# Product keys folded into the query's weights ahead of time, beside the token mixers

## Chip, core and metric

One core of a Trainium2 chip runs the kernel. The metric is the device time of one execution in microseconds (us), the median over several runs. PE is TensorE (PEld its weight loads), DVE VectorE, ACT ScalarE, POOL GpSimd, SP SyncE. SP, ACT and POOL issue DMAs, each from a queue of its own that works in program order; 16 DMA engines move the bytes.

## What is computed

One trunk layer on 1024 tokens of 1024 channels, float32. Two causal mixers (an RG-LRU and an S5) read one projection of the normalized input, their joint output is projected and added to the residual, and a product-key expert layer (PEER) follows:

```python
def block(xb):                                   # 128 tokens of the normalized h
    q = (xb @ wq).reshape(TOK_BLOCK, 8, 256)     # 8 heads, two halves of 128
    s1 = einsum('thd,kd->thk', q[..., :128], k1) # 128 keys each
    s2 = einsum('thd,kd->thk', q[..., 128:], k2)
    v1, i1 = top_k(s1, 16)
    v2, i2 = top_k(s2, 16)
    sc, cidx = top_k(all pairs v1 + v2, 16)
    e = expert numbers of the 16 pairs; g = softmax(sc)
    act = gelu(einsum('thkd,td->thk', u_tab[e], xb))
    return einsum('thk,thkd->td', g * act, v_tab[e])
```

For one half, `s = (xb @ wq_n) @ k.T`, which is also `xb @ (wq_n @ k.T)`: the product of the weights with the keys does not depend on the tokens.

## The kernel before

Products that need float32 accuracy are made of three matmuls in a faster type: a tile x is split into a high part (a rounded copy, made by ACT) and a low part (x less the high part, made by DVE), and low x high, high x low and high x high are summed in PSUM.

The program has four stages. **Mixers** (`front`, to about 250 us): input projection (`usp`, `pj`), S5 by quarters (`quarter`), the LRU heads (`lru`), then the GLU. Weights of the projection come in through SP's queue, nine pairs of parts ahead (`WBUFS`); two tiles `T0` hold the S5 kernel matrices; POOL clears them once at the start and does nothing until it loads the residual `h` for the output projection (L841). **Output projection** (`w_out`, `wop`), which also normalizes `h` for the expert layer (`Norm2`). **Query** (`query`, L1016): the tokens are 3 gathered blocks (TG = 384 tokens) and 5 dense blocks (TD = 640). For each of 16 column tiles of wq, first for the gathered blocks and then again for the dense ones, a 512 KB tile `wqr` is loaded by SP and split into `wqh` and `wql`; 24 matmuls (`qp`) of 384 columns, or 48 of 320, give the query in channel-by-token form, ACT copies it (`qt`), and for each block and half a float32 matmul with the keys `kT` gives the scores (`sp`). The first tile is made earlier, in `query0` (L880). Scores of the gathered blocks stay on chip (`sc`), those of the dense blocks go to DRAM (`S_d`) and are loaded back as `s` by `topk`. DVE's `top16` (MAX, MAX_INDEX, MATCH_REPLACE) finds 16 of 128 (`vg`, `ixg` for gathered blocks; `v`, `ix` for dense ones), then 16 pairs (`cd`, `scv`, `ci`).
**Experts**: for the gathered blocks, POOL fetches 128 rows of u and 128 of v for each block by indirect DMA (`row`), and DVE multiplies them with the tokens; the rows needed are spread over the rest of the program. For the dense blocks, all 128 x 128 experts are computed: tiles of u are loaded and split (`ur`, `uh`, `ul`), `ap` is the first matmul, `gp` builds the weights from one-hot products, `vp` is the second matmul.

The order of the work is decided when the program is built. Each strand (`proj`, `quarter`, `lru`, `query`, ...) is a generator that yields between pieces, and `Merge` (`mg`) runs the one whose modelled time plus a bias is least; `mg.at(t)` sets a strand's earliest time, `mg.dma(kb)` models a load, `mg.flag` and a yielded name let one strand wait for another. Each engine then carries out its instructions in the order that results, and an instruction whose operand isn't there holds up all that stand behind it on its engine. `fps` is the PSUM pool of `front`: 4 banks `pt`, 2 `pj`, 2 `pu`.

Of the kernel before, what the change touches and what calls it, by code (L numbers as in the profile page):

```python
# [149 lines left out]
def front(tc, a, cst, nd, mg):  # L150
# [28 lines left out]

    pvt = pools.open("fvt")  # L180
# [41 lines left out]
    pw = pools.open("fw", "right", bufs=9)  # L222
# [8 lines left out]
    WBUFS = 9  # L231
# [257 lines left out]
    def quarter(q):  # L489
# [42 lines left out]
        T0 = T0s[q % 2]  # L532
# [99 lines left out]
    mg.run([(0.5, proj_first())], until="us0")  # L632
# [26 lines left out]
    def lru(m):  # L659
# [18 lines left out]
        tau = pl.tile([P, T], F32, name="tau", tag="tau")  # L678
# [23 lines left out]
        V.tensor_tensor(tau, tau, i_, ALU.mult)  # L702
        yield
        V.tensor_tensor_scan(x, r_, tau, 0.0, ALU.mult, ALU.add)
# [93 lines left out]
    def wo_half(half):  # L798

        for n in range(2):  # L800
            for k in range(4):
                if half:
                    yield "half0" if (n, k) >= (1, 2) else "cols0"
                r = po.tile([P, 512], F32, name="wor", tag="wor", bufs=2)
                nc.sync.dma_start(r, a["w_out"][(4 * half + k) * P:(4 * half + k + 1) * P, 512 * n:512 * n + 512])
                wh = po.tile([P, 512], F32R, name="woh", tag="woh", bufs=10)
                wl = po.tile([P, 512], F32R, name="wol", tag="wol", bufs=10)
# [70 lines left out]
    nx = Norm2(tc, a, cst, pools, h, ss, mg)  # L878

    def query0():  # L880

        hi, lo = [], []
        for i in range(2):
            r = po.tile([P, 512], F32, name="wor", tag="wor", bufs=2)
            nc.sync.dma_start(r.rearrange("p (k n) -> p k n", n=P), a["wq"][0][:, 4 * i:4 * i + 4])
            yield "half0"
            wh = po.tile([P, 512], F32R, name="woh", tag="woh", bufs=10)
            wl = po.tile([P, 512], F32R, name="wol", tag="wol", bufs=10)
            S.activation(wh, r, AF.Copy)
            V.tensor_tensor(wl, r, wh.bitcast(F32), ALU.subtract)  # L890
            hi += [wh[:, k * P:(k + 1) * P] for k in range(4)]
            lo += [wl[:, k * P:(k + 1) * P] for k in range(4)]
            yield
        yield "xg"
        yield "half1"
        p_ = pt("qp")[:, :TG]
        for k in range(8):
            PE.matmul(p_, hi[k], nx.xGl[:, k], start=(k == 0), stop=False)
            PE.matmul(p_, lo[k], nx.xGh[:, k], start=False, stop=False)
            PE.matmul(p_, hi[k], nx.xGh[:, k], start=False, stop=(k == 7))  # L900
        yield
        S.activation(nx.q0, p_, AF.Copy)
        mg.flag("query0")
# [958 lines left out]
```

## Time and profile before

| | us |
|---|---|
| median of 3 runs (2582.36 to 2586.19) | 2584.22 |
| the profiled execution | 2589.38 |
| its span, first to last instruction | 2587.6 |

The profile is of one execution. Busy times are of matmuls in a pipeline whose ends are modelled, so a busy PE isn't PE at its peak: two matmuls overlap, and the step from one to the next is shorter than the duration listed. A group's row reads: line, engine, operation, out<-in, shapes, count, busy us, mean ns of one, idle time of the engine just before them and what ended most of it. L146 is the helper that records all compute instructions, so groups are told apart by their tiles. In the chain, each row is a start, a length and what ran, followed back from the last instruction. DMA share is the mean busy share of the 16 engines. The mean granted clock of PE over the span was 0.991.

### The profile page before, as it was taken

How to read it: one execution, taken by the hardware profiler on the slowest of the kernel's cores; microseconds unless marked ns; L12 is line 12 of the kernel's file. 1: busy time of each engine (PE TensorE's matmuls, PEld its weight loads, DVE VectorE, ACT ScalarE, POOL GpSimd, SP SyncE). 2: the span in 40 equal slices, each digit the busy share in tenths (PEclk: the TensorE clock that was granted, in tenths of full speed). 3: DMA queues.
4: the chain of work that ended last, by engine and by line, in shares of the span. 5: the costliest groups of instructions: out<-in, count | busy, mean ns of one | idle time of the engine just before them, and what ended most of it. 6: DMA issues, size and time to landing. Idle time of an engine off the chain costs nothing.

```text
span 2587.6 us, 40757 instructions
## 1 busy us (share of the span) xinstructions
PE 2493.5 (96%) x14623; PEld 2255.7 (87%) x14623; DVE 2364.6 (91%) x4556; ACT 1331.8 (51%) x2402; POOL 1149.4 (44%) x785
## 2 busy tenths in 40 slices
PE   7998999998999999999999999999999999999997
PEld 6776778998999999999999988888888888888886
DVE  7899559997999999999977599999999999999998
ACT  5566434332467777777877444334443443334442
POOL 0000000243466465574655365555556566555551
PEclk9999999998999999999999999999999999999999
DMA  5113223586799999998999999999999999999994
GB/s 180 35 42 100 72 92 123 178 289 234 275 364 347 345 337 361 348 327 310 355 380 345 343 382 359 355 359 351 350 350 373 349 357 355 355 353 351 348 355 152
DMA packets 303354, 752.78 MB, mean 291 GB/s; under 512 B 29872, under 2 KB 128368, under 8 KB 298416
## 3 DMA queue, kind: packets, MB, share of 16 engines
q0 software_dynamic: 111744, 406.90, 43.1%
q1 hardware_dynamic: 186576, 336.28, 36.4%
q10 hardware_dynamic: 4832, 7.00, 0.8%
q8 instruction: 115, 1.88, 0.3%
q14 instruction: 87, 0.71, 0.1%
HBM read 662.92 MB, written 85.98 MB: 289 GB/s over the span
## 4 chain that ended last, share of the span: by engine, by line
PE 60%; DVE 20%; issue 3%; DMA 2%; ACT 1%; POOL 1%; another core or an unknown queue 0%; DVEq 0%; SPq 0%; ACTq 0%; POOLq 0%
PE vp L146 26%; PE ap L146 19%; PE total L146 6%; PE qp L146 4%; DVE row L146 3%; PE gp L146 3%; DVE hb L146 3%; DVE ul L146 2%; DVE oh L146 2%; DVE ix L146 1%; DVE ohA L146 1%; DVE v L146 1%; PE wop L146 1%; DVE s L146 1%; DVE ci L146 1%
## 5 line engine op out<-in xcount | busy, mean ns | idle before, releaser
L1290 POOL DMA_INDIRECT row<-in_peer_u_dram,idx x384 | 579.1, 1508 | 691.8 <-DVE scv L146 268.7
L1290 POOL DMA_INDIRECT row<-in_peer_v_dram,idx x384 | 563.1, 1466 | 452.8 <-DVE hb L146 278.7
L146 PE MATMUL ap<-xDl,uh 128*128 128x320 f32 x2048 | 647.8, 316 | 5.0 <-ACT aa L146 5.0
L146 PE MATMUL ap<-xDh,ul 128*128 128x320 f32 x2048 | 639.6, 312 | 8.8 <-DVE ul L146 8.6
L146 PE MATMUL ap<-xDh,uh 128*128 128x320 f32 x2048 | 636.9, 311 | 0.0
L146 DVE SCALAR_TENSOR_TENSOR hb<-row,act,hb 128x1024 f32<-128x1024 f32 x384 | 494.9, 1289 | 4.9
L146 DVE CUSTOM_DVE_ANT_0 row<-row,xg 128x1024 f32<-128x1024 f32 x384 | 459.0, 1222 | 4.3 <-DMA row<-in_peer_u_dram,idx 4.3
L146 PEld LDWEIGHTS ap<-xDh,ul 128*128 128x128 f32 x2048 | 388.7, 190 | 11.9 <-DVE ul L146 10.8
L146 PE MATMUL vp<-vl,hh 128*128 128x512 f32 x1024 | 398.7, 389 | 0.0
L146 PE MATMUL vp<-vh,hl 128*128 128x512 f32 x1024 | 398.5, 389 | 0.0
L146 PE MATMUL vp<-vh,hh 128*128 128x512 f32 x1024 | 398.5, 389 | 0.0
L146 PEld LDWEIGHTS ap<-xDl,uh 128*128 128x128 f32 x2048 | 388.5, 190 | 7.8 <-ACT aa L146 6.6
L146 PEld LDWEIGHTS ap<-xDh,uh 128*128 128x128 f32 x2048 | 388.2, 190 | 0.0
L146 ACT ACTIVATE gq<-gt 128x640 f32<-128x640 f32 x128 | 174.7, 1365 | 319.1 <-DVE hr L146 253.7
L146 PEld LDWEIGHTS vp<-vh,hh 128*128 128x128 f32 x1024 | 192.2, 188 | 40.2
L146 PEld LDWEIGHTS vp<-vl,hh 128*128 128x128 f32 x1024 | 192.2, 188 | 39.4 <-issue 0.4
L146 PEld LDWEIGHTS vp<-vh,hl 128*128 128x128 f32 x1024 | 192.2, 188 | 38.8
L146 ACT ACTIVATE ohB<-ohB,kt 128x128 f32<-128x128 f32 x480 | 202.1, 485 | 0.0
L146 ACT ACTIVATE aa<-ap 128x320 f32<-128x320 f32 x194 | 84.4, 435 | 207.9 <-PE ap L146 198.7
L146 PE MATMUL gp<-ohB,ohA 128*128 128x128 f32 x1280 | 173.1, 278 | 15.7 <-DVE ohB L146 13.8
L146 PEld LDWEIGHTS gp<-ohB,ohA 128*128 128x128 f32 x1280 | 159.2, 192 | 25.4 <-issue 13.1
L146 DVE TENSOR_TENSOR ul<-ur,uh 128x1024 fp32r<-128x1024 f32 x128 | 156.6, 1224 | 21.2 <-ACT uh L146 21.2
(445 smaller groups left out, 4500.2 us busy)
## 6 DMA issues: line engine op xcount, KB each, us to landing
ur<-in_uT_dram SPq DMA_DIRECT2D x128, 512.0 KB
vr<-in_peer_v_dram SPq DMA_DIRECT2D x128, 512.0 KB
gt<-G_d SPq DMA_DIRECT2D x32, 1280.0 KB
G_d<-gs SPq DMA_DIRECT2D x79, 512.0 KB
A_d<-aa SPq DMA_DIRECT2D x96, 320.0 KB
hr<-A_d SPq DMA_DIRECT2D x96, 320.0 KB
wqr<-in_wq_dram SPq DMA_DIRECT2D x31, 512.0 KB
row<-in_peer_u_dram,idx POOLq DMA_INDIRECT x384
```

The costliest lines, as they stand in the source:

```text
L146: return fn(*args, **kw)
L1290: G.indirect_dma_start(out=r, out_offset=None, in_=a["peer_v" if at >= P else "peer_u"], in_offset=bass.IndirectOffsetOnAxis(ap=idx[n][:, ...
```

## The change

The keys are multiplied into the query's weights once, by a new strand `fold` that runs beside the mixers. It takes the transposed weights in 32 units of 256 KB (128 query channels by 512 input channels). For each unit a tile `wqr` (two buffers) is loaded through POOL's queue, four float32 matmuls with `kT` give `fo` (512 columns), ACT copies the high part into `wqh` (one buffer), DVE writes the low part over `wqr`, and POOL's queue stores both into `W_d` in DRAM. `BEAT` is the distance of two units in the builder's time.

```diff
+    def fold():
+        kT = pfo.tile([P, 2, P], F32, name="kT")
+        nc.gpsimd.dma_start(kT, a["kT"])
+        units = [(n, i) for n in range(16) for i in range(2)]
+        ready = []
+        def load():
+            n, i = units[len(ready)]
+            r = pfo.tile([P, 512], F32, name="wqr", tag="wqr", bufs=2)
+            nc.gpsimd.dma_start(r, a["wqT"][n][:, 512 * i:512 * i + 512])
+            ready.append((r, mg.dma(256)))
+        load()
+        for at, (n, i) in enumerate(units):
+            if at + 1 < len(units):
+                load()
+            r, t = ready[at]
+            mg.at(t + 1.0)
+            yield
+            t = mg.cur["t"]
+            p_ = pu("fo")
+            for j in range(4):
+                PE.matmul(p_[:, j * P:(j + 1) * P], r[:, j * P:(j + 1) * P], kT[:, n % 2], start=True, stop=True)
+            yield
+            hi = pfo.tile([P, 512], F32R, name="wqh", tag="wqh")
+            lo = r.bitcast(F32R)
+            S.activation(hi, p_, AF.Copy)
+            V.tensor_tensor(lo, p_, hi.bitcast(F32), ALU.subtract)
+            yield
+            for m, x in enumerate((hi, r)):
+                nc.gpsimd.dma_start(nx.W_d[m, n // 4, :, n % 4, 4 * i:4 * i + 4].bitcast(F32),
+                                    x.bitcast(F32).rearrange("p (k n) -> p k n", n=P))
+            mg.at(t + BEAT)
+            yield
+        mg.flag("fold")
-    mg.run([(0.5, proj_first())], until="us0")
+    mg.run([(0.5, proj_first()), (FOLD, fold())], until="us0")
```

The query then gives scores at once: tokens are the stationary side, and a quad of four column tiles (two heads, 512 scores) the moving one, so each of 768 matmuls has 512 columns; `sp`, `qt` and the split leave the stage. Its weights come from `W_d` by SP, a high and a low tile of 1 MB for half of the input channels of a quad, one step ahead; `query_head` does the first half quad on tiles loaded during the output projection. Scores of a block leave as 512 columns (`S_d`, 256 KB).

```diff
-                        for k in range(8):
-                            PE.matmul(p_, wh[:, k], dl[:, k, sl], start=(k == 0), stop=False)
-                            PE.matmul(p_, wl[:, k], dh[:, k, sl], start=False, stop=False)
-                            PE.matmul(p_, wh[:, k], dh[:, k, sl], start=False, stop=(k == 7))
-                        if i == 0 and at < 31:
-                            nxt = weights(at + 1)
...
-                    for f in range(2):
-                        PE.matmul(p_[:, f * P:(f + 1) * P], qs[f][:, n * P:(n + 1) * P], kT[:, f], start=True, stop=True)
...
+            for c in range(4):
+                held = nx.held if part + c == 0 else [nx.bank() for _ in blocks]
+                for j in range(1 if part + c == 0 else 0, 2):
+                    load()
+                    wh, wl = ready.pop(0)
+                    for n, b in enumerate(blocks):
+                        for k in range(4):
+                            nx.term(held[n], dh, dl, n, 4 * j + k, wh[:, :, k], wl[:, :, k])
                         yield
...
+                        if j:
+                            sc = pq.tile([P, 512], F32, tag="sc", name="sc", bufs=3)
+                            S.activation(sc, held[n], AF.Copy)
+                            if part:
+                                nc.sync.dma_start(S_d[b, :, 2 * c:2 * c + 2], sc.rearrange("p (h k) -> p h k", h=2))
```

To make room, the mixers keep one `T0` instead of two, eight weight pairs ahead instead of nine, eight `woh`/`wol` buffers instead of ten, and `lru` uses the tiles of `x` and `xc` for `tau` and `x`. PSUM pool `fps` stays open until the query is done.

```diff
-    WBUFS = 9
+    WBUFS = 8
-    T0s = [p5.tile([P, 8, P], F32, name=f"T0{i}") for i in range(2)]
-    for x in T0s:
-        G.memset(x, 0.0)
+    T0 = p5.tile([P, 8, P], F32, name="T0")
+    G.memset(T0, 0.0)
-        tau = pl.tile([P, T], F32, name="tau", tag="tau")
+        tau, x = x, xc
```

How it stands on the engines. POOL's queue during the mixers, before (`T0` are the cleared tiles, `h` the residual's blocks):

```order
L146 MEMSET T00_538 128x1024
L146 MEMSET T01_539 128x1024
L841 DMA h7_2457<-in_x_dram 128x1024
L841 DMA h6_2456<-in_x_dram 128x1024
L841 DMA h5_2455<-in_x_dram 128x1024
```

and now, the first units of the fold (`wqr_550`, `_625` and `_552`, `_682` are the same two buffers in turn):

```order
L635 DMA kT_548<-in_kT_dram 128x256
L642 DMA wqr_550<-in_wqT_dram 128x512
L642 DMA wqr_552<-in_wqT_dram 128x512
L146 MEMSET T0_546 128x1024
L662 DMA W_d_97<-wqh_570 128x512
L662 DMA W_d_97<-wqr_550 128x512
L642 DMA wqr_625<-in_wqT_dram 128x512
L662 DMA W_d_97<-wqh_632 128x512
L662 DMA W_d_97<-wqr_552 128x512
L642 DMA wqr_682<-in_wqT_dram 128x512
```

The load of a third unit now stands between the stores of the first and those of the second, and it can't start before the store of the first unit's `wqr` has left; the eight loads of `h` stand behind the last store.

DVE in the first half of the query stage, before, where the low parts of the weights stand between the searches of the gathered blocks:

```order
L146 MAX vg_3360<-sc 128x8 x2
L146 MAX_INDEX ixg_3361<-vg_3360,sc 128x8 x2
L146 TENSOR_TENSOR wql<-wqr,wqh 128x1024
L146 MAX vg_3362<-sc 128x8 x2
L146 MAX_INDEX ixg_3363<-vg_3362,sc 128x8 x2
L146 MATCH_REPLACE sc<-vg_3362,sc 128x128 x2
L146 MAX vg_3362<-sc 128x8 x2
L146 MAX_INDEX ixg_3363<-vg_3362,sc 128x8 x2
L146 TENSOR_TENSOR wql<-wqr,wqh 128x1024
```

and DVE now in the mixers, where the fold's low part has come between the S5 and LRU instructions:

```order
L146 TENSOR_TENSOR wqr<-fo,wqh 128x512
L146 SCALAR_TENSOR_TENSOR xa_74<-r__1143,i__1144 128x1024
L146 SCALAR_TENSOR_TENSOR xc<-xa_75,cols,xc 128x1024
L146 TENSOR_TENSOR wqr<-fo,wqh 128x512
L146 SCALAR_TENSOR_TENSOR xc<-xa_75,cols,xc 128x1024 x2
L146 TENSOR_TENSOR Wr<-inr,Ec 128x4x127
L146 TENSOR_TENSOR xt<-ini,Es 128x4x127
```

The 31 full-width `wql` have left the query stage, and 32 half-width `wqr` stand among the mixers.

SP's queue at the end of the query stage, before:

```order
L1023 DMA wqr<-in_wq_dram 128x1024 x2
L1067 DMA S_d<-sc 128x256 x5
L1023 DMA wqr<-in_wq_dram 128x1024
L1067 DMA S_d<-sc 128x256 x10
L1115 DMA s<-S_d 128x2048
```

and now:

```order
L1068 DMA wq_5199<-W_d 128x4x512
L1090 DMA S_d<-sc 128x512
L1068 DMA wq_5197<-W_d 128x4x512
L1090 DMA S_d<-sc 128x512
L1140 DMA s<-S_d 128x2048
L1090 DMA S_d<-sc 128x512 x4
```

The first dense block's scores `s` are now read back ahead of the stores of the other four blocks.

More of the change, by code (lines that the diff above doesn't have):

```diff
@@ L178, in front @@
     S.dma_start(cols, a["cols"])
+    nx = Norm2(tc, pools)
+    pfo = pools.open("ffold")
     pvt = pools.open("fvt")
@@ L701, in lru @@
         yield
-        V.tensor_tensor(tau, tau, i_, ALU.mult)
+        V.tensor_tensor(i_, tau, i_, ALU.mult)
         yield
-        V.tensor_tensor_scan(x, r_, tau, 0.0, ALU.mult, ALU.add)
+        V.tensor_tensor_scan(tau, r_, i_, 0.0, ALU.mult, ALU.add)
         yield
@@ L877, in front, with bank, query_head @@
     pools.close("fa")
[L878 to L893, printed above, removed]
+    nx.open(a, cst, pools, h, ss, mg)
+    used = [0]
+    def bank():
+        used[0] += 1
+        return (pt if used[0] % 6 < 4 else pj)("qp")
+    nx.bank = bank
+    def query_head():
+        yield "fold"
+        w = []
+        for m in range(2):
+            x = pvt.tile([P, 4, 4, P], F32R, name="wq0", tag="Vt", bufs=2)
+            nc.sync.dma_start(x.bitcast(F32), nx.W_d[m, 0, :, :, 0:4].bitcast(F32))
+            w.append(x)
         yield "xg"
         yield "half1"
-        p_ = pt("qp")[:, :TG]
-        for k in range(8):
[L898 to L903, printed above, removed]
+        nx.held = [bank() for _ in range(NG)]
+        for n, p_ in enumerate(nx.held):
+            for k in range(4):
+                nx.term(p_, nx.xGh, nx.xGl, n, k, w[0][:, :, k], w[1][:, :, k])
+            yield
+        mg.flag("head")
     def norm2_g():
@@ L1012, in norm2_d, with load @@
     def norm2_d():
-        yield from nx.run(dblocks, xDh, xDl, pt)
+        yield from nx.run(dblocks, xDh, xDl, nx.pu)
         mg.flag("xd")
     def query():
-        kT = pq.tile([P, 2, P], F32, name="kT", bufs=1)
-        S.dma_start(kT, a["kT"])
-        def weights(n):
-            wr = pq.tile([P, 8, P], F32, tag="wr", name="wqr")
-            nc.sync.dma_start(wr, a["wq"][n % 16])
-            wh = pq.tile([P, 8, P], F32R, tag="wh", name="wqh")
-            wl = pq.tile([P, 8, P], F32R, tag="wl", name="wql")
-            split_to(wh, wl, wr)
-            return wh, wl
-        nxt = weights(1)
+        quads = [(part, c, j) for part in range(2) for c in range(4) for j in range(2)][1:]
+        ready = []
+        def load():
+            if quads:
+                _, c, j = quads.pop(0)
+                w = []
+                for m, tag in enumerate(("wh", "wl")):
+                    x = pq.tile([P, 4, 4, P], F32R, name="wq2", tag=tag)
+                    nc.sync.dma_start(x.bitcast(F32), nx.W_d[m, c, :, :, 4 * j:4 * j + 4].bitcast(F32))
+                    w.append(x)
+                ready.append(w)
+        load()
         yield
         for part, (blocks, dh, dl) in enumerate(((gblocks, nx.xGh, nx.xGl), (dblocks, xDh, xDl))):
-            nt = len(blocks) * P
-            nsp = -(-nt // 512)
-            w = nt // nsp
             if part:
@@ L1491, in peer @@
     mg.run([(1.0, topks()), gr], until="q")
+    pools.close("fps")
+    ppa = pools.open("ppa", bufs=2, space=PSUM)
+    ppt = pools.open("ppt", bufs=2, space=PSUM)
     mg.run([], until="chosen")
```

83 lines of the change are left out of this document (34 added, 49 removed).

## The prediction

> **What bounds the kernel now.** First the page's busy times, then the busy time of each engine by stage (stretch in us, its length, then PE, PEld, DVE, ACT, POOL busy, granted clock, DMA share, GB/s), since one share over the whole span mixes stages.
>
> ```profile
> PE 2493.5 (96%) x14623; PEld 2255.7 (87%) x14623; DVE 2364.6 (91%) x4556; ACT 1331.8 (51%) x2402; POOL 1149.4 (44%) x785
> ...
> 50.00:228.00 178.00, 163.78 (x1073) 127.60 (x1071) 166.79 (x290) 107.62 (x164) 0.00 (x0) 0.98 0.15 38
> 250.00:371.00 121.00, 113.37 (x505) 91.51 (x504) 65.54 (x98) 43.69 (x64) 2.52 (x5) 0.97 0.24 88
> 371.00:611.00 240.00, 228.67 (x1498) 220.84 (x1497) 212.93 (x800) 85.00 (x164) 61.97 (x44) 0.99 0.61 207
> 605.00:1050.00 445.00, 425.98 (x2941) 416.95 (x2940) 437.54 (x1250) 288.32 (x680) 236.06 (x152) 0.98 0.90 321
> 1050.00:1440.00 390.00, 383.24 (x2753) 379.23 (x2752) 350.50 (x746) 303.75 (x736) 229.65 (x140) 1.00 0.97 347
> 1440.00:2588.00 1148.00, 1130.05 (x5583) 977.71 (x5582) 1076.62 (x1230) 459.60 (x516) 614.57 (x433) 0.99 0.93 344
> ```
>
> The mixers (50 to 228) keep PE busy for 163.8 of 178 us and DVE for 166.8: both are nearly full, POOL does nothing, and DMA moves 38 GB/s. The output projection (250 to 371) is PE's. The query stage (371 to 611) is shared by PE and DVE; DVE has 27 us free in it. From 605 to 1050 DVE is full (437.5 of 445), and from there to the end PE is. The order in which DVE stands is the same in both kernels from the 25th expert tile on, so a shift that DVE has when it reaches that stage goes through to the end. The question is therefore how much later the mixers end and how much shorter the query stage becomes. The chain of work that ended last shows where the query stage goes (start us, us, what):
>
> ```profile
> 352.03 19.07 PE wop L146 x84
> 371.11 3.92 DMA wqr<-in_wq_dram
> ...
> 454.12 7.30 PE qp L146 x42
> ...
> 493.29 1.14 DVE wql L146
> ...
> 499.43 4.45 DMA row<-in_peer_u_dram,idx
> ...
> 554.61 13.06 PE qp L146 x89
> 567.66 0.89 PE sp L146 x8
> ...
> 602.33 3.46 DMA S_d<-sc
> 605.86 5.13 DMA s<-S_d
> ```
>
> The stage begins with a wait for the first weights (371.11), which could only be loaded when the projection had left its buffers. In its first half the low parts of the weights (wql) stand among the top-16 searches on DVE; in the second PE runs alone, and at its end DVE waits 8.6 us until the scores have gone to DRAM and come back.
>
> **The query stage: what goes.** Matmul steps come from that chain: 512 columns 19.07/84 = 0.227 us, 384 columns 7.30/42 = 0.174, 320 columns 13.06/89 = 0.147, and a record of a score matmul 0.89/8 = 0.111. Before: 384 x 0.174 + 768 x 0.147 = 179.7 us of projection. After: 768 x 0.227 = 174.3. So the projection stays, and the 128 score matmuls (two records each) leave:
>
> ```profile
> L146 PE MATMUL sp<-kT,qt 128*128 128x128 f32 x250 | 38.6, 284 | 3.1 <-ACT qt L146 2.1 <-ACT sc L146 1.0
> ...
> L146 DVE CUSTOM_DVE_ANT_0 row<-row,xg 128x1024 f32<-128x1024 f32 x36 | 43.4, 1225 | 2.8 <-DMA row<-in_peer_u_dram,idx 2.8
> L146 DVE TENSOR_TENSOR wql<-wqr,wqh 128x1024 fp32r<-128x1024 f32 x31 | 37.7, 1217 | 4.6 <-ACT wqh L146 4.5
> ```
>
> With the 6 of the first tile these are 256 records x 0.111 = 28.4 us of PE. DVE loses 31 wql at a step of 1.14 = 35 us, and 7 of the 36 gathered rows move behind the stage (29 stand ahead of the first dense search in the new order), 7 x 1.22 = 8.5 us that are paid back in the DVE-bound stage. What is left: PE 174.3 + 40 transposes x 0.11 = 179 us, DVE 213 - 35 - 8.5 = 169 us.
>
> New here are the loads. A step takes two tiles of 1 MB (2.1 MB together), twice the bytes of before. For the gathered blocks a step lasts 36 x 0.227 = 8.2 us, and 2.1 MB at 347 GB/s (stretch 1050:1440) take 6.0, with some 3 until they land (the 4.45 of a gathered row of 512 KB less 1.5 for its bytes): about 1 us is missing at each of 7 steps, so PE ends at 179 + 8 = 187 us after 371. For the dense blocks (480 matmuls, 109 us) the DMA engines must move 16.8 MB of weights, 5.2 MB of scores and 29 to 36 rows of 0.52 MB: 37 to 41 MB, 107 to 118 us at 347 GB/s. I take it that the rows, not the weights, are late, and that DVE comes to the first dense search 10 us after PE's end, at 197. The wait for S_d nearly goes: block 0's scores are stored and read back while PE still works on four blocks. Before, that search began at 611, 240 us in: **-43 us**, and +8.5 for the rows. Bounds: -53 (DVE there when PE ends) to -32 (41 MB at the 321 GB/s of 605:1050, 128 us after the first 80).
>
> **The mixers: what comes.** 32 units: 4 matmuls (8 records x 0.111 = 0.89 us), one high part on ACT, one low part on DVE, three DMAs on POOL's queue. The nearest rows for the two parts read PSUM in the same form, 128x512:
>
> ```profile
> L146 DVE TENSOR_TENSOR xDl<-x2t,xDh 128x512 fp32r<-128x512 f32 x10 | 6.8, 676 | 0.0
> L146 ACT ACTIVATE xDh<-x2t 128x512 fp32r<-128x512 f32 x10 | 5.9, 596 | 4.4 <-PE x2t L146 4.3
> ```
>
> PE gets 32 x 0.89 = 28.5 us, DVE 32 x 0.6 to 0.68 = 19 to 22, ACT 19 (it has 70 free). PE had 14 us free from 50 to 228, DVE 11. So the least is 28.5 - 14 = +14 us on PE (DVE: 19 - 11 = +8), the work being pushed into every gap.
>
> On top comes the round of a buffer. A unit's low part is written over its raw tile, so the tile is free for the load two units on only when the store of the low part has left, and POOL's queue holds that load with the next unit's stores behind it. A round is a load (4.45 us for 512 KB from the chain, 3.7 less the time of half its bytes), 0.89 + 0.60 + 0.68, and a store (3.46 in the chain): 9.3 to 10.1 us; I take 10. What stands between the low parts on DVE, each instruction at its step, which is about 0.08 less than these durations:
>
> ```profile
> L146 DVE SCALAR_TENSOR_TENSOR xc<-xa,cols,xc 128x1024 f32<-128x1024 f32 x12 | 15.3, 1275 | 0.0
> L146 DVE TENSOR_TENSOR wl<-wr,wh 128x256 fp32r<-128x256 f32 x36 | 14.9, 423 | 2.8 <-ACT wh L146 2.8
> ...
> L146 DVE TENSOR_TENSOR WB<-ta,tb 128x512 f32<-128x512 f32 x6 | 4.2, 692 | 0.0
> ```
>
> comes to 183 us for 31 gaps, 11.8 us for two units on average, but from 7.0 to 18.5; 12 of the 30 pairs hold less than 10. Walking through them, no unit earlier than a round after the one two before it, the waits add up to 4 us for a round of 9, 11 for 10, 19 for 11, 28 for 12, 38 for 13. With the 11 of a round of 10 the mixers end 14 + 12 = **+26 us** later. Bounds: +14 (no wait) to +42 (a round of 12).
>
> The rest I cost at nothing: one T0 tile instead of two (the next quarter's first write follows the last quarter's read in PE's order anyway), eight weights ahead instead of nine (36 wl waited 2.8 us in all), tau in the tile of x (the next head's convolution may have to wait for one more ACT instruction, with other work of DVE at hand), h loaded behind the last fold store (the last fold matmul stands 56 projection matmuls, 12.7 us, ahead of the first GLU matmul). The head of the query now runs on tiles loaded during the projection; that is the 5 us of the wait at 371, within the 43.
>
> Sum: +26 - 43 + 8.5 = **-8.5 us**. The profiled execution took 2589.38 us (span 2587.6), the median of the runs is 2584.22; taken from the median, 2575.7, or 2576.
>
> **A rule against it.** How fast POOL's queue issues beside a full DVE is seen twice (a stretch of the engines, and two DMAs of POOL):
>
> ```profile
> 240.00:250.00 10.00, 9.26 (x41) 7.09 (x40) 10.00 (x10) 9.64 (x12) 1.90 (x4) 1.00 0.69 233
> ...
> 241.78 1.80 POOL L841 DMA_DIRECT2D h<-in_x_dram  x3 [203.22 <-PE pj L146]
> ...
> 510.52 2.82 POOL L1290 DMA_INDIRECT row<-in_peer_u_dram,idx  x1 [0.30 <-DVE ib L146]
> ```
>
> Three plain loads took 0.6 us each while DVE was busy for 10.00 of 10 us; a gather was stretched to 2.82. Were all 96 DMAs of the fold stretched like that gather, POOL would need 3 x 2.82 + 3.46 for the store to land, 11.9 us a unit, 381 us for 32 where there are 178, and the kernel would take about 2584 + 203 - 34 = 2753. The Trainium skill (SBUF — State Buffer, the trap box ahead of "A bandwidth-pool intuition that's wrong") says that a DMA issued by GpSimd cannot write its descriptors while VectorE holds the port the two share, and gives about 620 ns alone and 3100 ns beside a copy. The 0.6 us of h agree with the first, the gather's 2.82 come near the second. Since the plain form is the fold's, this rival gets 0.03.
>
> **Rivals.**
> - Slower: the round through POOL's queue. If the two buffers take 13 us for a round (an ACT or DVE queue that holds each unit up by another 1.5 us), the waits are 38 instead of 11: +18 us, 2602. It decides from a round of 11.1 us (waits of 20); beyond 11.7 the kernel is measurably slower. For it: 12 tight pairs, and the parts stand behind scans and 128x1024 instructions. Against: the mean pair has 11.8. 0.20.
> - No change: gathers and weights share the DMA engines at 321 GB/s instead of 347, the query stage gives -32 only: +26 - 32 + 8.5 = +2.5, 2587. For it: that rate is the stage's that follows. 0.17.
> - Faster still: the waits fall into gaps that are there, +14, and DVE is there when PE ends, -53: -30, 2554. For it: 27 us of free DVE before. Against: 41 MB in 118 us. 0.13.
> - The forecast, -18 to -2: 0.47. With the 0.03 above that is all.
>
> The range takes in the third and most of the first: 2554 to 2604. What a measurement can tell from no change is about 0.2%, 5 us: of the forecast 0.38 is faster and 0.09 the same; of the first rival 0.16 slower, 0.04 the same; of the second 0.12 the same, 0.05 slower. Faster 0.51, the same 0.25, slower 0.24.
>
> **What would show it.** Right: the last wop at about 397 instead of 371; low parts of the fold waiting for ACT, ACT for PE, PE for wqr by some 11 us in all, mostly in the tight pairs; no wql, no sp; the first dense v at 594 (611 - 17), with no wait for s worth speaking of where the chain had 8.6 us; the 25th ul 8 us earlier, and equal gaps from there on. Wrong: PE waiting for wqr by over 20 us (the round), PE's qp waiting for wq tiles by over 15 us (the loads), a mean POOL issue in the mixers above 1.5 us (the port), or a wait for h at the first combine.

## The result and the profile after

| | us |
|---|---|
| before, median of 4 runs | 2583.29 |
| the change, median of 4 runs (2603.96 to 2609.06) | 2606.31 |
| ratio | 1.0082, 95% interval 1.0068 to 1.0096 |
| the profiled execution of the change (span 2606.1) | 2607.81 |

The change makes the kernel slower by 0.8%, where 0.3% faster was forecast. The busy times by stage, for the change (stretch, its length, PE, PEld, DVE, ACT, POOL busy, granted clock, DMA share, GB/s):

```profile
50.00:228.00 178.00, 162.66 (x1154) 132.32 (x1154) 156.80 (x279) 107.63 (x169) 40.67 (x75) 0.98 0.47 148
291.00:409.00 118.00, 112.07 (x504) 90.88 (x503) 61.47 (x93) 41.32 (x60) 0.00 (x0) 0.97 0.27 96
409.00:614.00 205.00, 186.55 (x800) 150.76 (x799) 169.24 (x755) 29.48 (x50) 49.53 (x37) 0.95 0.79 294
```

In the first row nothing has become fuller: PE is as busy as before (162.7 of 178 us, before 163.8) and DVE is less so (156.8, before 166.8). The mixers have taken up the fold (28.5 us of PE by the forecast) and have become longer, with as much idle time as before. In the third row, the query stage, PE has gaps and the clock is 0.95; it had been 0.99.

Four points of time tell where the 18.4 us between the two spans came from (start or end in us from the span's start). The medians are 23.0 us apart: the profiled execution of before is 6 us above its median, that of the change 1.5.

| | before | change | difference |
|---|---|---|---|
| first wop starts | 250.6 | 291.5 | +40.9 |
| last wop ends | 371.1 | 409.1 | +38.0 (forecast +26) |
| first dense v | 611.0 | 614.2 | +3.1; the query stage is 34.9 shorter (forecast 43) |
| end of the span | 2587.6 | 2606.1 | +18.4; 15.3 lost behind the first v (forecast 8.5) |

The waits of the mixers (0 to 291.5 us; engine, tile, what it waited for: us in all, times, longest):

```profile
PE usp L146 <- DVE wl L146: 13.6, 5, 10.2
...
ACT wqh L146 <- PE fo L146: 43.7, 12, 6.1
...
DVE wqr L146 <- ACT wqh L146: 11.0, 10, 4.9
PE fo L146 <- DMA wqr<-in_wqT_dram: 10.6, 11, 1.8
...
PE glp L146 <- DVE gl L146: 6.7, 1, 6.7
```

PE's wait for the two buffers is there, in the size forecast (10.6 us). Beside it DVE waits 11.0 us for the fold's high parts, ACT 43.7 for its matmuls, and PE 6.7 for the input `gl` of the GLU, for which it had waited 0.7 before. In the query stage (405 to 622):

```profile
DVE v L146 <- DMA s<-S_d: 20.4, 1, 20.4
PE qp L146 <- DMA wq<-W_d: 15.3, 3, 7.4
...
DVE row L146 <- DMA row<-in_peer_u_dram,idx: 0.7, 1, 0.7
```

PE waited 15.3 us for weights, DVE 0.7 for a gathered row. The chain of the change, from the projection to the first dense search (start, length, what):

```profile
390.70 18.41 PE wop L146 x81
...
549.93 13.60 DMA wq<-W_d
...
563.58 15.53 PE qp L146 x60
...
580.22 19.83 DMA wq<-W_d
...
600.10 5.24 PE qp L146 x12
...
608.42 5.72 DMA s<-S_d
```

Two tiles of weights took 13.6 and 19.8 us to land, and the 12 matmuls after the second wait took 0.437 us each instead of 0.227. The granted clock (third from the end of each row) shows why:

```profile
559.00:563.50 4.50, 0.00 (x0) 0.00 (x0) 4.50 (x18) 0.31 (x1) 3.25 (x2) 1.00 1.05 393
563.50:567.00 3.50, 3.42 (x9) 2.73 (x10) 3.50 (x13) 0.00 (x0) 2.26 (x3) 0.56 1.05 397
568.00:578.00 10.00, 10.00 (x45) 8.26 (x44) 10.00 (x16) 2.40 (x4) 7.11 (x5) 1.00 1.03 393
592.50:600.00 7.50, 0.19 (x1) 0.00 (x0) 1.27 (x3) 0.00 (x0) 2.70 (x3) 0.64 1.03 405
600.00:604.00 4.00, 3.90 (x9) 3.17 (x10) 0.00 (x0) 0.00 (x0) 0.00 (x0) 0.50 0.29 115
```

The half clock sets in at the end of the first wait and about 2 us into the second (0.64 is the mean of its 7.5 us), and it lasts for some 3 to 5 us of work, so these waits are paid about 1.4 times. The Trainium skill (TensorE: Matmul & The Clock Gate, Part 1) says that an idle window of about 3.4 us halves the clock until PE has been busy for as long; the slow matmuls behind these two waits, of 4.6 and 7.4 us, agree. Shorter waits, of about 2 us, halved it too, which that sentence doesn't give; they stand in the last section.

This makes an account of PE's time possible for every run: its idle time, what it lost to the half clock (half of the time in which it worked at a clock of 0.5), and the rest, which is steps of matmuls. The tables below use it.

### The profile page after: what moved, and what is told of

Its sections match the earlier page's. It is cut to its first block, busy times and chain, and to the rows that moved or that the text cites. A ratio compares the mean times of both kernels' runs of the same rounds, so it can differ in the third digit from the quotient of the medians.

```text
span 2606.1 us, 40068 instructions
## 1 busy us (share of the span) xinstructions
PE 2493.4 (96%) x14239; PEld 2224.8 (85%) x14239; DVE 2348.0 (90%) x4555; ACT 1299.1 (50%) x2324; POOL 1206.0 (46%) x881
## 4 chain that ended last, share of the span: by engine, by line
PE 60%; DVE 15%; DMA 4%; issue 4%; POOL 1%; ACT 1%; SPq 0%; DVEq 0%; POOLq 0%; ACTq 0%
PE vp L146 26%; PE ap L146 18%; PE total L146 6%; PE qp L146 5%; DVE hb L146 3%; PE gp L146 3%; DVE row L146 3%; DVE ul L146 2%; DVE ix L146 1%; DMA wq<-W_d 1%; POOL row L1315 1%; DVE ohA L146 1%; PE wop L146 1%; DVE v L146 1%; DVE s L146 1%
## 5 line engine op out<-in xcount | busy, mean ns | idle before, releaser
L1315 POOL DMA_INDIRECT row<-in_peer_u_dram,idx x384 | 568.4, 1480 | 678.1 <-DVE act L146 244.8
L1315 POOL DMA_INDIRECT row<-in_peer_v_dram,idx x384 | 578.8, 1507 | 442.6 <-DVE hb L146 279.3
L146 DVE SCALAR_TENSOR_TENSOR hb<-row,act,hb 128x1024 f32<-128x1024 f32 x384 | 492.5, 1283 | 12.2 <-DMA row<-in_peer_v_dram,idx 7.3
L146 PEld LDWEIGHTS ap<-xDh,ul 128*128 128x128 f32 x2048 | 389.2, 190 | 12.3 <-DVE ul L146 11.2
L146 PE MATMUL gp<-ohB,ohA 128*128 128x128 f32 x1280 | 172.6, 278 | 19.5 <-DVE ohB L146 16.2
L146 PEld LDWEIGHTS gp<-ohB,ohA 128*128 128x128 f32 x1280 | 158.7, 191 | 29.9 <-issue 12.8
L146 DVE TENSOR_TENSOR ul<-ur,uh 128x1024 fp32r<-128x1024 f32 x128 | 155.9, 1219 | 21.7 <-ACT uh L146 21.6
```

What stands on the lines that cost most here:

```text
L146: return fn(*args, **kw)
L1315: G.indirect_dma_start(out=r, out_offset=None, in_=a["peer_v" if at >= P else "peer_u"], in_offset=bass.IndirectOffsetOnAxis(ap=idx[n][:, ...
```

## The experiments

Each is the change with one thing altered, if nothing else is said. The expectations weigh two theories of the mixers: by the work theory PE had no gaps that the fold could use, by the round theory the waits for a raw tile's buffer set the pace. "Ratio" is the time against the kernel before, run beside it; the change itself, run again:

> The change itself once more, as the mark for the next run on the same chip. Time 2604 to 2612, 0.6 to 1.0% above the kernel before; first wop 290 to 301, query stage (last wop to first dense v) 203 to 207 us.

Ratio 1.0077 (1.0064 to 1.0090), 2606.55 us. Last wop at 413.4, query stage 208.0 us, and 5.6 us instead of 15.3 lost behind the first v. So single points of one profile move by 5 to 10 us while the time stays; the times have more weight in what follows.

### What the mixers paid for

**The smaller buffers alone**, in the kernel before:

```diff
-    WBUFS = 9
+    WBUFS = 8
-    T0s = [p5.tile([P, 8, P], F32, name=f"T0{i}") for i in range(2)]
+    T0 = p5.tile([P, 8, P], F32, name="T0")
-        tau = pl.tile([P, T], F32, name="tau", tag="tau")
+        tau, x = x, xc
```

> The kernel before with the smaller buffers of the change alone: one T0, eight weight pairs ahead, tau in the tile of x (no fold, the old query). If these cuts cost nothing, as the prediction had it, the last wop ends at 371 us as before (within 2) and the time is 2583 (within 4). If they are a part of the 38 us by which the mixers grew, the last wop ends 8 us or more later and the time is above 2590.

Ratio 0.9987 (0.9970 to 1.0005): they cost nothing, as the prediction had it. The last wop came at 362.4, not within 2 us of 371 as expected, but in an execution of 2574.33 us where the median is 2585.76. So the mixers' end can move by some 8 us even without a fold. The eight `woh`/`wol` buffers of the change are not in this run.

**The fold's work left out, its stores kept:**

```diff
-            if at + 1 < len(units):
-                load()
-            r, t = ready[at]
+            if at:
+                for m, x in enumerate(parts):
+                    nc.gpsimd.dma_start(nx.W_d[m, n // 4, :, n % 4, 4 * i:4 * i + 4].bitcast(F32),
+                                        x.bitcast(F32).rearrange("p (k n) -> p k n", n=P))
+                mg.at(mg.cur["t"] + BEAT)
+                yield
+                continue
+            r, t = ready[0]
```

> The change with the fold's work left out: only the first unit is computed, and its two parts are stored to all 32 places (the scores are those of a wrong matrix). The 64 stores stay, 31 loads, 31 units of matmuls, high and low parts go. Both theories of the mixers (work on a full PE; waits for the two buffers) expect the last wop at 371 to 375 us instead of 409, and with a query stage that is still 205 us a time of 2606 - 36 = 2570. If smaller buffers or the stores' DMA traffic cost something, it ends above 380.

Ratio 0.9945 (0.9929 to 0.9962), 35 us under the change: that is the price of the fold's work and waits. The last wop ended at 379.8, 5 us later than expected. The stores were issued without pace, all by 94 us, and ACT waited 32.3 us for loads of w_in (17.7 in the change), so what the stores cost in the change itself can't be read from this run.

**PE's work alone, a quarter of it kept:**

```diff
-            for j in range(4):
-                PE.matmul(p_[:, j * P:(j + 1) * P], r[:, j * P:(j + 1) * P], kT[:, n % 2], start=True, stop=True)
+            PE.matmul(p_[:, 0:P], r[:, 0:P], kT[:, n % 2], start=True, stop=True)
+            p_ = p_.rearrange("p (a b) -> p a b", b=P)[:, 0:1, :].to_broadcast([P, 4, P])
```

> The change with one of a unit's four fold matmuls, whose 128 columns are read four times by ACT and DVE: 32 x 0.67 = 21 us of PE are left out (the scores are those of a wrong matrix), the loads, high and low parts, stores and buffers are as in the change. Work theory (PE had no gaps that the fold could use, so its 30.6 us came out in full): the last wop 16 to 21 us earlier, at 388 to 393, time about 2588. Round theory (the waits for a buffer set the pace): at most 6 us earlier, above 403, time above 2600.

Ratio 1.0060 (1.0035 to 1.0084), about 5 us under the change, first wop at 291.6 as in the change. 21 us of PE's work went, and the time hardly moved. Its waits in the mixers, and its stretch from 50 to 228 us, say where they went:

```profile
PE fo L146 <- DMA wqr<-in_wqT_dram: 18.8, 12, 3.1
```

```profile
50.00:228.00 178.00, 150.60 (x973) 119.86 (x972) 147.33 (x263) 101.44 (x161) 40.90 (x75) 0.90 0.47 146
```

PE waits longer for raw tiles (18.8 us; 10.6 and 11.4 in the change's two profiles), its idle time in all is 13 us longer, and its clock in this stretch is 0.90, where the change had 0.98 and 0.94.

**The low parts alone left out:**

```diff
-            V.tensor_tensor(lo, p_, hi.bitcast(F32), ALU.subtract)
-            for m, x in enumerate((hi, r)):
+            for m, x in enumerate((hi, hi)):
```

> The change with the low parts left out: the high part is stored twice (the scores lose accuracy). DVE loses 22 us, and a raw tile comes free when PE has read it, so the waits for wqr (10.6 us of PE) go too. Work theory: PE keeps its 30.6 us, the last wop is 8 to 12 us earlier, at 397 to 401, time about 2596. If DVE is what bounds the mixers: 20 us or more earlier, below 389, time below 2587. Round theory: about 25 us earlier, at 384, since nothing waits any more.

Ratio 1.0115 (1.0087 to 1.0142): slower than the change, which no theory had. The high part is now stored twice from its one buffer, and ACT waits for that:

```profile
ACT wqh L146 <- DMA W_d<-wqh: 33.9, 14, 5.5
```

So the run put a new wait in place of the DVE work and can't tell what DVE alone is worth. The first wop came at 290.1, as in the change; the time was lost in the projection, which took 133 us instead of 118 at a clock of 0.89.

**The loads left out, and the low part in a tile of its own:**

```diff
-            if at + 1 < len(units):
-                load()
-            r, t = ready[at]
+            r, t = ready[0]
...
-            lo = r.bitcast(F32R)
+            lo = pfo.tile([P, 512], F32R, name="wql", tag="wql", bufs=1)
```

> The change with the loads of the fold left out: every unit multiplies the first raw tile (the scores are those of a wrong matrix), and low parts go to a tile of their own. All matmuls, high and low parts and stores stay; no wait for wqr is left. Round theory: the first wop 10 to 18 us earlier (274 to 282), time about 2592. If the wait for wqr is only where the time shows that the mixers' engines lose to one another anyway: within 4 us, 2602 or above.

Ratio 1.0048 (1.0032 to 1.0064), 8 us under the change; first wop at 290.9 (the change 291.5 and 295.8). No PE wait for wqr is left, but the round theory's 10 to 18 us at the first wop aren't there: idle time fell by only 4 to 6 us, others taking the place of these waits. ACT's wait for fold matmuls fell from 43.7 to 6.6 us as well, so it isn't what makes the mixers longer either.

**Both, a quarter of the matmuls and no loads:**

> The change with one of four fold matmuls and without the loads (both as in the runs before; the scores are those of a wrong matrix): PE's 21 us and the waits for raw tiles go together, high and low parts and stores stay. If work and waits stand in for one another, which is why neither alone moved anything: the first wop at 275 or earlier, time 2585 or less. If each is worth only what it was alone (6 and 9 us by the times): 282 to 288, time about 2591. If the 22 us of DVE hold the mixers by themselves: 289 or later, 2598 or above.

Ratio 1.0001 (0.9987 to 1.0016), 20 us under the change, more than the 5 and the 8 of the two alone; first wop at 280.7 (in spite of 15.4 us lost to the clock). It lies between the two numbers expected, by the time nearer to the first, by the first wop to the second. That PE's work and the waits for raw tiles stand in for one another is likely but not shown: 20 is 7 more than 5 + 8, and the intervals of the four ratios leave about 9 open.

**Twice the matmuls:**

```diff
-            for j in range(4):
+            for j in (0, 1, 2, 3) * 2:
```

> The change with every fold matmul done twice (the same scores): 28.5 us more of PE, all else as it was. If PE's work comes out in full in the mixers: the first wop 24 to 34 us later than the change's 291 to 301, so 318 to 332, time 2630 to 2640. If there are gaps that take it, as the prediction had it for half of the fold: at most 14 us later, below 312, time below 2622.

Ratio 1.0141 (1.0121 to 1.0160), 16 us over the change. The first wop came at 316.5, 25 us later; 7 of these came back in the projection, and in the mixers PE's idle time fell by 10. The first wop fits work that comes out in full (24 to 34 us later), the time only just fits gaps that take it (2621.97, below 2622). So of added work a part does go into gaps; that this is so because the others now wait for PE is a guess.

PE's account up to the first wop (us):

| | first wop | idle | of it for wqr | lost to half clock | steps |
|---|---|---|---|---|---|
| before | 250.6 | 31.8 | | 3.4 | 215.4 |
| before, smaller buffers | 243.0 | 28.2 | | 0 | 214.8 |
| the change | 291.5 | 40.3 | 10.6 | 4.6 | 246.5 |
| the change again | 295.8 | 38.8 | 11.4 | 11.5 | 245.5 |
| a quarter of the matmuls | 291.6 | 53.8 | 18.8 | 13.7 | 224.2 |
| no loads | 290.9 | 34.7 | 0 | 12.4 | 243.8 |
| both | 280.7 | 43.2 | 0 | 15.4 | 222.1 |
| stores alone | 262.5 | 39.9 | 0 | 8.4 | 214.2 |
| twice the matmuls | 316.5 | 30.4 | 11.2 | 5.7 | 280.5 |

The steps follow the work to within 3 us everywhere: the fold is 31 us. The idle time doesn't shrink when the fold comes: without the waits for wqr it is 29.7 and 27.4 us, and was 31.8 and 28.2. A part of it lies where no fold matmul could stand, so here it is by stretches (us):

| | up to 39, where the fold begins | from there to the last pj | of it ahead of fold matmuls | last pj to first wop |
|---|---|---|---|---|
| before | 15.1 | 16.0 | | 0.7 |
| before, smaller buffers | 12.8 | 14.1 | | 1.2 |
| the change | 13.6 | 20.0 | 12.2 | 6.7 |
| the change again | 13.3 | 19.0 | 11.8 | 6.6 |
| a quarter of the matmuls | 13.6 | 34.5 | 21.7 | 5.8 |
| no loads | 12.6 | 16.3 | 1.1 | 5.8 |
| twice the matmuls | 12.8 | 17.6 | 13.2 | 0 |

The second stretch, for before, the change, and the change without loads (columns as above):

```profile
39.00:241.50 202.50, 186.52 (x1193) 146.42 (x1192) 187.10 (x317) 124.86 (x195) 0.00 (x0) 0.98 0.17 45
39.00:275.20 236.20, 216.19 (x1433) 173.99 (x1432) 202.88 (x343) 140.84 (x223) 50.99 (x94) 0.99 0.46 143
39.00:275.00 236.00, 219.70 (x1426) 178.70 (x1426) 201.39 (x342) 142.14 (x221) 34.80 (x64) 0.95 0.36 110
```

In the change the mixers' own gaps shrank from 16.0 to 7.8 us there, but 12.2 us of waits ahead of fold matmuls came in their place; without the loads these are gone and the own gaps are back at 15.2. At the end PE waits some 6 us more for `gl`.

**Three other ways to run the fold.** First a raw tile of its own and one for the low part, with the load issued behind the matmuls that free the tile, so that no load waits for its unit's store:

```diff
-            r = pfo.tile([P, 512], F32, name="wqr", tag="wqr", bufs=2)
+            r = pfo.tile([P, 512], F32, name="wqr", tag="wqr", bufs=1)
...
-            if at + 1 < len(units):
-                load()
...
+            if at + 1 < len(units):
+                load()
...
-            lo = r.bitcast(F32R)
+            lo = pfo.tile([P, 512], F32R, name="wql", tag="wql", bufs=1)
```

> The change with the low part in a tile of its own (one buffer) and one raw tile instead of two, in the same memory: a raw tile comes free when PE has read it, not when its low part has reached DRAM, so a load no longer stands behind a store. Round theory (the waits for wqr, 10.6 us on PE, and the half-clock stretches behind waits): PE waits below 4 us for wqr, the first wop 7 to 15 us earlier than the change's 291.5, time 2592 to 2599. If only PE's 30.6 us of matmuls matter: no more than 3 us earlier, 2603 or above. If one raw tile is worse than two: waits above 10.6 us, 2608 or above.

Ratio 1.0089 (1.0056 to 1.0122). With one raw tile PE waited 14.1 us for it instead of 10.6: the load begins sooner but has less time. Then units further apart:

```diff
-FOLD, BEAT = 1.0, 8.5
+FOLD, BEAT = 1.0, 11.0
```

> The change with the fold's units 11 instead of 8.5 units of the builder's time apart, so that the last 7 of 32 units stand in the output projection and the others have more time for a round. Round theory: PE waits below 4 us for wqr in all, the last wop 8 to 14 us earlier than the change's 409, time about 2595. If the fold's price is PE's work alone, which is the same wherever it stands: within 4 us, 2602 to 2610.

Ratio 1.0120 (1.0090 to 1.0150). The first wop came 7 us earlier with 7.7 us of waits, and the projection gave back 22: 140 us instead of 118, at a clock of 0.88 (the change 0.97).

```profile
284.00:424.00 140.00, 126.67 (x536) 103.56 (x537) 64.30 (x97) 44.18 (x64) 5.97 (x11) 0.88 0.29 105
```

Last, units started earlier:

```diff
-    mg.run([(0.0, us_first()), (0.0, squares()), (2.0, setup())], until="x")
+    mg.run([(0.0, us_first()), (0.0, squares()), (2.0, setup()), (FOLD, fold())], until="x")
```

> The change with the fold's strand started beside the norm and the first projection instead of behind them: units begin some 5 us earlier, stand about 4 units ahead throughout, and the last one is done before the last projection matmuls. If the end of the mixers is late because the last low parts stand ahead of the GLU's inputs on DVE (PE waited 6.7 us for gl): that wait below 2 us and the first wop 5 to 10 us earlier, time about 2598. If the mixers' length is the sum of PE's work and waits wherever they stand: within 3 us, 2603 to 2610.

Ratio 1.0162 (1.0142 to 1.0181). The wait for gl went (0.5 us), but the waits for wqr rose to 17.3, fold matmuls waited for DVE (3.6 us for z, 2.9 for wl), and PE stood idle for 7.1 us ahead of the first wop, for which the profile shows no releaser: first wop at 308.9. All three expectations of a gain fell; the fold's price changes its place and does not shrink.

### Why the weights came late

**Stores of the scores from ACT's queue**, so that loads on SP's queue don't stand behind them:

```diff
-                                nc.sync.dma_start(S_d[b, :, 2 * c:2 * c + 2], sc.rearrange("p (h k) -> p h k", h=2))
+                                nc.scalar.dma_start(S_d[b, :, 2 * c:2 * c + 2], sc.rearrange("p (h k) -> p h k", h=2))
```

> The change with the stores of the dense scores issued from ACT's queue, so that no load of a weight tile on SP's queue stands behind a store that waits for ACT. If the late weights (15.3 us of PE waiting, and a clock halved for 19.3 us) come from SP's order, which held two loads for 6 and 8 us: waits for wq fall to 8 us or less, the first dense v is 8 to 12 us earlier, time about 2597. If they come from the DMA engines shared with the gathers: waits of 12 us or more, time 2603 or above.

Ratio 1.0075 (1.0051 to 1.0098); PE waited 13.8 us for wq. SP's order isn't the cause.

**Fewer gathers in the stage:**

```diff
-    pace[0] = 3.0
+    pace[0] = 5.0
```

> The change with the gathers of the query stage spaced 5 instead of 3 units of the builder's time: 20 rows instead of 29 stand before the first dense v, so 4.7 MB less are moved beside the weights, and 9 x 1.14 = 10 us of DVE are paid back later. If the gathers are what delays the weights: waits for wq below 6 us, the first dense v 12 to 20 us earlier (594 to 602), the 25th ul 2 to 10 us earlier, time about 2598. If SP's order is the cause: waits of 12 us or more, the first v where it was, and the time about 2614, later by the rows.

Ratio 1.0104 (1.0082 to 1.0126). With 9 rows less, PE still waited 12.2 us and the query stage was 3 us shorter; the rows were paid later. The number of gathers is not it either: while they run, they fill the DMA engines as before.

**The low tiles from ACT's queue, the high ones from SP's:**

```diff
-                    nc.sync.dma_start(x.bitcast(F32), nx.W_d[m, c, :, :, 4 * j:4 * j + 4].bitcast(F32))
+                    (nc.scalar if m else nc.sync).dma_start(x.bitcast(F32), nx.W_d[m, c, :, :, 4 * j:4 * j + 4].bitcast(F32))
```

> The change with the low tiles of the weights loaded from ACT's queue and the high ones from SP's, so that three queues instead of two ask the DMA engines while the gathers run. If each queue gets a share: waits for wq below 8 us instead of 15.3, the first dense v 8 to 14 us earlier relative to the last wop (191 to 197 us after it), time about 2597. If it is only the bytes: waits of 12 us or more, time 2603 or above; if ACT is held up by the waiting loads, the scores' copies come late and PE waits for a bank: above 2608.

Ratio 1.0080 (1.0061 to 1.0099), 18.6 us of waits. A second queue doesn't help; the low tiles on ACT's took 13.2 us to land in the median.

**Pieces of 8 KB instead of 2 KB**, by the layout of the folded weights in DRAM:

```diff
-        self.W_d = dr.tile([2, 4, P, 4, 8, P], F32R, name="W_d")
+        self.W_d = dr.tile([2, 4, 2, P, 4, 4, P], F32R, name="W_d")
```

> The change with the folded weights laid out in DRAM so that a tile of 1 MB is 8 KB in one piece for each partition, not four pieces of 2 KB. In the change's stretch from 500 to 610 us SP's queue moved 16.84 MB in 8648 packets (1.95 KB each) and the gathers' queue 19.40 MB in 5328 (3.64 KB). If the weights come late because their packets are the smaller ones beside the gathers: packets of SP's queue above 3 KB, waits for wq below 6 us instead of 15.3, the first dense v 10 to 17 us earlier relative to the last wop (188 to 195 us after it instead of 205), time about 2594. If it is only the bytes: waits of 12 us or more, 203 to 207 us, time 2603 or above.

Ratio 1.0071 (1.0052 to 1.0090). The DMA view from 500 to 610 us, for the change (packets, MB, share of the 16 engines; q0 carries the gathers, q1 the weights) and its median time of a weight tile to landing:

```profile
q0 software_dynamic: 5328, 19.40, 45.6%
q1 hardware_dynamic: 8648, 16.84, 41.6%
...
wq<-W_d SPq DMA_DIRECT2D x12, 1024.0 KB, 10.2
```

and with pieces of 8 KB:

```profile
q0 software_dynamic: 5289, 19.30, 46.0%
q1 hardware_dynamic: 4470, 18.85, 44.4%
...
wq<-W_d SPq DMA_DIRECT2D x12, 1024.0 KB, 8.2
```

The weights' packets grew from 1.95 to 4.2 KB, above the gathers' 3.6; tiles land in 8.2 us instead of 10.2, PE waits 3.5 us instead of 15.3, and the first dense v comes 193.6 us after the last wop instead of 205.1. So the size of the pieces is what made the weights late. Why is less clear. The Trainium skill (DMA: Bandwidth & Descriptors, Queues, rings and completion order) says that each DMA engine takes its queues in turn, a whole packet from each. By that rule the queue with the smaller packets gets the smaller share. The larger packets did move more in the same stretch (18.85 MB instead of 16.84), but two things don't come from that rule alone. A second queue for the weights should then have helped as well, and it didn't. And from 415 to 500 us, where no gather runs, the tiles with pieces of 8 KB landed faster too (the change, then this layout):

```profile
wq<-W_d SPq DMA_DIRECT2D x18, 1024.0 KB, 7.6
```

```profile
wq<-W_d SPq DMA_DIRECT2D x18, 1024.0 KB, 6.8
```

So 0.8 us of a tile have nothing to do with the gathers; beside them it is 2.0.

The time, however, fell by less than expected. It was run again beside the change:

> The change with the weights' 8 KB layout once more, beside the change. If the query stage's gain reaches the end, the time is 9 to 13 us below the change's in the same rounds, about 2596, with a query stage of 192 to 196 us and waits for wq below 6 us. If the gain of the one profile was the difference between two profiles: within 3 us of the change.

Ratio 1.0060 (1.0044 to 1.0076), 2604.13 us beside 2606.55. Query stage 198.9 us with 6.4 us of waits for wq, but the first wop at 308.4 (300.9 in the first run of it; 291 to 297 in the five profiles of the change's own mixers). The profiled execution took 2614.9, so 308.4 is likely on the high side. What the query gained, the mixers gave back. In both profiles the fold's stores landed later. The DMA view from 60 to 270 us, of the change (2.4 and 2.9 in its second profile) and of this layout (3.1 and 3.4 in its first):

```profile
W_d<-wqh POOLq DMA_DIRECT2D x29, 256.0 KB, 2.7
W_d<-wqr POOLq DMA_DIRECT2D x29, 256.0 KB, 2.8
```

```profile
W_d<-wqh POOLq DMA_DIRECT2D x27, 256.0 KB, 3.3
W_d<-wqr POOLq DMA_DIRECT2D x27, 256.0 KB, 3.6
```

PE's waits for wqr were 12.8 and 17.6 us in them. To tell this from chance, the partitions' pieces were spaced 9 KB apart instead of 8:

```diff
-        self.W_d = dr.tile([2, 4, 2, P, 4, 4, P], F32R, name="W_d")
+        self.W_d = dr.tile([2, 4, 2, P, 18, P], F32R, name="W_d")
```

> The 8 KB layout with 1 KB left free behind each partition's piece. If the round of a unit's buffer sets the mixers' waits and the stores' landing is a part of it: with stores back at 2.8 us the first wop comes at 291 to 297 with 10 to 14 us of waits for wqr, the query stage stays at 192 to 199 us, time about 2596; with stores still at 3.3 us or more the first wop stays at 301 or later. If the mixers of the two runs before were long by chance, the first wop is at 291 to 297 with stores at 3.3 us.

Ratio 1.0024 (1.0012 to 1.0036), 2593.31 us. The stores are back, with the first wop at 295.5, and the query stage stays short, at 195.7 us:

```profile
W_d<-wqh POOLq DMA_DIRECT2D x29, 256.0 KB, 2.6
...
W_d<-wqr POOLq DMA_DIRECT2D x28, 256.0 KB, 2.8
```

This takes back 14 of the change's 20 us and is the best version with the fold; it is still 0.2% slower than the kernel before. It is also 10 us faster than the layout 8 KB apart, clear of the intervals, so the spacing matters. That it acts through the round of the buffers is not shown: PE waited 12.1 us for wqr here, and 12.8 in the first run 8 KB apart. PE's account of the query stage (last wop to first dense v, us):

| | length | idle | of it for wq | lost to half clock | the rest |
|---|---|---|---|---|---|
| before | 239.9 | 11.3 | | 1.7 | 226.9 |
| the change | 205.1 | 18.4 | 15.3 | 6.7 | 179.9 |
| stores from ACT's queue | 204.9 | 17.7 | 13.8 | 6.8 | 180.4 |
| fewer gathers | 202.1 | 16.2 | 12.2 | 5.4 | 180.5 |
| two queues | 206.1 | 20.7 | 18.6 | 3.4 | 182.0 |
| pieces of 8 KB | 193.6 | 10.5 | 3.5 | 1.5 | 181.6 |
| the same, 9 KB apart | 195.7 | 11.2 | 3.2 | 3.1 | 181.4 |

In the last two PE also waited, at the end, for ACT to copy out the last scores (5.9 and 6.3 us in all); the matmul steps are the same, 180 to 182 us, in every version with the fold.

## Why the prediction was wrong

- **The mixers, +26 forecast, +38 in the profile.** The step that failed is "So the least is 28.5 - 14 = +14 us on PE", with "the work being pushed into every gap". The 28.5 us were nearly right (31 in the account), and so were the 11 us of waits for the two buffers (10.6). But the 14 us of gaps weren't room: PE's idle time apart from the waits for wqr went from 31.8 to 29.7, so 2 us were gained, not 14. Where the fold runs, the 16 us of gaps shrank by 8, but the fold's matmuls brought 12 us of waits with them, which the 11 us of the forecast had counted on top of filled gaps; and a term was missing, the 6 us that PE now waits for `gl` at the end. Of the rest, 1 us more was lost to the half clock (8 in the second profile) and 3 came back in the projection. Why the gaps stay is shown in part. PE alone doesn't set the mixers' length: 21 us less of its work left the first wop where it was, with 13 us more of idle time. Nor do the waits for raw tiles: without them the own gaps came back. That PE, ACT and DVE wait in order for each other, so that an instruction put into one engine's gap holds up what the others wait for, fits this, but no run shows it by itself. One result stands against it: when the fold's matmuls were doubled, PE's idle time fell by 10 us.
- **The round of a buffer.** Right in size, but the rival that made a slow kernel of it (13 us a round, 38 of waits, 2602) isn't what happened, though its time is near: PE waited 10.6 us. Leaving all waits for raw tiles out gained 8 us.
- **The query stage, -43 forecast, -34.9 in the profile.** The failing step is "I take it that the rows, not the weights, are late". The matmul steps were right (180 us with the transposes, forecast 179). The bytes were not what failed, but who waits for them: rows came in time (DVE waited 0.7 us), and PE waited 15.3 us for weights where about 8 were allowed. Their pieces of 2 KB were the reason: in pieces of 8 KB the wait was 3.2 to 6.4 us. And a term was missing: after a wait PE starts at half its clock, 6.7 us instead of 1.7. "PE's qp waiting for wq tiles by over 15 us" had been named as a sign against it.
- **The wait for S_d.** It was said nearly to go; DVE waited 20.4 us for s, since PE's late last weights held the last head's scores of block 0 too.
- **The 7 rows, +8.5.** 15.3 us were lost behind the first v in the one profile and 5.6 in the other of the same kernel, so the size stands between them; it can't be settled closer by these.
- **Edits costed at nothing.** Right as far as it was run: 0.9987 with the smaller buffers of the mixers.
- **POOL's queue beside a full DVE.** The rival of a stretched issue fell. Loads and stores of the fold, all beside DVE at 88% (count, minimum, median and maximum in ns):

```profile
L642 POOL DMA_DIRECT2D wqr<-in_wqT_dram x32: 541/541/589, 2.2 to 253.3; - x32
...
L662 POOL DMA_DIRECT2D W_d<-wqr x32: 539/539/882, 43.2 to 267.2; - x32
```

  One of them was stretched, to 0.88 us. The 3.1 us that the Trainium skill (SBUF — State Buffer, A bandwidth-pool intuition that's wrong) gives for a DMA of GpSimd beside a VectorE copy did not appear with this kernel's DVE instructions.
- **The sum.** +38.0 - 34.9 + 15.3 = +18.4 us in the two profiles (+23.0 by the medians) against a forecast of -8.5; the time lies 2 us above the range, whose upper end allowed for a slower round but not for the mixers and the query stage falling short together.

What the prediction could have seen: the score matmuls that leave the query (28.4 us by its own count) and the fold's that enter the mixers (28.5) are the same amount of PE's work. The change could gain on PE only if the mixers had room for the fold, and that was the term taken on trust.

Left open: which wait holds the mixers' gaps open, what the high and low parts cost by themselves (leaving out the low ones brought a new wait), and a fold with three or more raw tiles, for which there is no memory in the mixers; it wasn't tried.

## What to carry to other kernels

Idle time in a stage where two engines are nine tenths busy and wait for each other in order need not be room for more work; count none of it until a run has shown it filled, and count the waits that the new work brings with it. Before moving work from one stage to another, set the same engine's time in both against each other: if it is equal, the gain must come from a wait that ends, and that wait has to be named. When a transfer shares the DMA engines with another, look at the size of its pieces as well as at its bytes.

## What the runs showed of the hardware

A PE wait of 2 us can already halve the clock for the 3.4 us that follow, though not each does. From the kernel before (first a wait of 2.1 us within 325.2 to 327.6 and what follows, then one of 2.4):

```profile
325.20:327.60 2.40, 0.32 (x3) 0.01 (x1) 2.21 (x8) 0.54 (x2) 0.00 (x0) 1.00 0.00 0
327.60:330.60 3.00, 3.00 (x7) 2.43 (x8) 0.59 (x1) 1.15 (x2) 0.00 (x0) 0.51 0.44 175
331.00:337.00 6.00, 6.00 (x27) 4.94 (x27) 1.50 (x2) 1.15 (x2) 0.00 (x0) 1.00 0.09 34
504.50:506.90 2.40, 0.03 (x1) 0.03 (x1) 2.40 (x8) 0.31 (x1) 2.10 (x2) 1.00 0.90 328
506.90:510.00 3.10, 3.10 (x21) 3.10 (x22) 3.10 (x15) 1.39 (x2) 2.49 (x3) 1.00 0.97 337
```

Seven matmuls filled 3.0 us at a clock of 0.51, where 27 filled 6.0 behind them. The starts of the half clock suggest why. In this profile they lie at 85.3, 221.8, 262.8 and 327.6 us, which is 40, 12 and 19 times 3.413 us apart, and each lasted 3.41 us; in the change's first profile 563.9 and 594.6 lie 9 times 3.413 apart. So the clock changes on a fixed grid of 3.41 us, and it should matter how a wait lies in it: of the 3.41 us that end at 327.6 PE was idle for 2.1, while the 2.4 us of the other wait fall on both sides of a point of the grid. That this is all that decides isn't shown. Which waits do it differs from one execution to the next: the change lost 4.6 us to the clock in its mixers in one profile and 11.5 in the other.

Stores of 256 KB whose partitions lie 8 KB apart in DRAM landed in 3.1 to 3.6 us (medians of two profiles), those 16 or 9 KB apart in 2.4 to 2.9 (three profiles), with the same pieces of 2 KB.
